# Hybrid S5 and pooling layer on one core: every queue position set anew, a head with identity transposes and halved loads

## The chip, the cores and the metric

The kernel runs on one core of one Trainium2 chip. The metric is the device time of one execution in microseconds (us); lower is better. The time before is 720.16 us, the median of three runs (717.47 to 720.93).

## The reference

One decoder layer over a prompt of 2048 tokens and 8 single-token samples, model width 1024. Cut to what matters:

```python
proj = h @ w_in                                  # 1024 -> 2048
s_in, s_gate, p_in, p_gate = jnp.split(proj, [512, 1024, 1536], axis=-1)
sy, hr, hi = _s5_mixer(s_in, ...)                # complex diagonal scan, 32 groups x 64 states
sy = gelu(sy)
sy = sy * sigmoid(sy @ glu_w + glu_b)
py, buf = _pool_mixer(p_in, ...)                 # trailing means over 2, 4, 8, 16 tokens, then a 128x128 map each
mixed = concat([sy * silu(s_gate), py * silu(p_gate)])
y = _layer_norm(alpha * h + mixed @ w_out, ln_g, ln_b)
```

All tensors are 32-bit floats. The kernel keeps the precision by splitting each matmul operand into a high and a low part (`hl`), so that a product takes three matmuls: high by high, and the two mixed ones.

## The kernel before, in words

All of the work sits in one function, `hybrid_step`. The tokens are worked in chunks of 512, 512, 512, 256 and 256 (plus the 8 samples); for the first two column blocks the chunks are finer (256, 256, 512, 512, 256, 256).

**Stages.** (1) The head: `load_x`/`put_x` (lines 506 and 522) load 128 tokens, transpose them on TensorE (8 transposes, line 147) into PSUM, ScalarE casts them to the high part `xh` (line 156) and VectorE subtracts for the low part `xl` (line 150). Two PSUM pairs (tag `pair`) take turns. `load_w`/`split_w` (lines 174 and 180) load and split 128 columns of `w_in`. (2) `proj(m, c)` (line 196) multiplies column block m (0 to 15) by a chunk: 24 matmuls into one bank. Blocks 0 to 3 are the SSM input (`u_tile`, line 533), 4 to 7 its gate, 8 to 11 the pooling input, 12 to 15 the pooling gate. (3) Beside it `params` (line 222) works out the SSM's constants from small loads: a long chain of short VectorE instructions, then eight rounds of two groups each in which VectorE forms the products `sp`, TensorE multiplies and transposes into `ps_ks`, and the results go to DRAM (`sw_d`, `qw_d`, `wt_d`). `tables` (line 460) builds rotation tables in four quarters, each of six doubling levels, four `tx` pairs and two stores; a quarter's tile must be stored before the next one's first memset. (4) `ssm_task` (line 662) runs 16 groups: rotate, scan, rotate back on VectorE, and short matmuls on TensorE; the outputs go to `y_d` in DRAM. (5) The pooling blocks: `pool_in`, `pool_diff` (adds on GpSimd, a difference `df` on VectorE, its split `dh`) and `pool_gate` with the matmuls `pm`. (6) `prep` reads `y_d` back and splits it (`yh`), `glu_chunk` multiplies by the GLU weights (line 1060), `out_tile` by `w_out` (line 1100), and the layer norm ends each 128 tokens; `out_last` is the last tile and has its own tail.

**What sets the order.** TensorE, ScalarE, VectorE and GpSimd are under a manual schedule (line 495): each engine runs its instructions in the order in which the program emits them. That order comes from the class `Line` (line 47). Its clock `line.t` is advanced by the planned TensorE time of the matmuls that are emitted (3n/2400 for three matmuls of n columns). Tasks are generators: where one says `yield 3.0`, it goes on when `line.t` has come 3.0 further, and what it then issues lands in the engines' queues between the matmuls emitted before and after. `line.finish(task)` jumps the clock forward until the task is done. So every `yield` number is a place in the queues and no wait on the chip; a number too small puts an instruction in front of others while its inputs are still missing, and the engine stands. SyncE's queue, which issues all DMAs, follows the same program order and waits for each DMA's inputs.

The places that the steps below touch: `PD` (line 544), the start of `params`; `PY` and `YS` (lines 490 and 491), the yields of a round of constants and of an SSM group; `x_task` (line 563), which puts the token tiles from the fourth on; `ssm_tail` (line 919), which starts when the SSM is done, and the `hook` (line 1016) that adds it at the second step of pooling block 11; the delays of `w_task` and `w_in_task` (lines 185 and 192).

## Time and profile before

| what | value |
|---|---|
| median of three runs | 720.16 us |
| the profiled execution: its own time | 722.89 us |
| its span, first to last instruction | 721.1 us |
| TensorE busy | 685.0 us, 95% |
| VectorE busy | 483.1 us, 67% |
| ScalarE / GpSimd busy | 237.2 / 189.2 us |
| mean granted TensorE clock | 0.984 |

The profile is one execution. "Busy" counts the time in which an engine had an instruction in work; the time that TensorE wasn't busy, about 36 us, is what a new order can give back, besides stretches at the lower clock. A row of a timeline gives the start, the duration and the number of merged instructions; in brackets stands the idle time of the engine before it and what ended it.

### The profile page before, as it was taken

Reading aid. Unit: us, or ns where it says so; the run is one execution under the profiler, and the core shown is the slowest. Engines: PE = TensorE matmul, PEld = TensorE weight load, DVE = VectorE, ACT = ScalarE, POOL = GpSimd, SP = SyncE. Lnnn points to the kernel's source line nnn. Section 1 sums busy time; section 2 is a strip of 40 time slices with the busy share of each in tenths; the row PEclk is TensorE's granted clock in tenths of the full one; section 3 lists DMA queues with packets and bytes.
Section 4 is the critical chain, followed back from the end, with each engine's and each line's share of the span. In section 5 each row is a group of like instructions: output and inputs, shape, how many; then the busy total and the mean of one; then the engine's idle time right before and its main releaser. Section 6 shows DMA issues by size and latency. Waiting matters only on the chain.

```text
span 721.1 us, 10754 instructions
## 1 busy us (share of the span) xinstructions
PE 685.0 (95%) x3735; PEld 579.2 (80%) x3735; DVE 483.1 (67%) x999; ACT 237.2 (33%) x487; POOL 189.2 (26%) x251
## 2 busy tenths in 40 slices
PE   6999997999999999999998999989999999999995
PEld 5988785887888888988986787777888868888884
DVE  3689969754466788789788853487554556656444
ACT  4343323322344443443433221254221323323100
POOL 1005534410000011121222313646313233151322
PEclk9999998999999999999999999999999999999998
DMA  8993675777645545354443224935455563634432
GB/s 278 231 336 91 163 202 146 178 187 221 195 149 159 166 116 154 126 155 146 138 146 114 81 67 134 322 113 125 113 118 129 136 159 78 148 88 117 116 88 59
DMA packets 137909, 107.95 MB, mean 150 GB/s; under 512 B 74435, under 2 KB 115559, under 8 KB 137847
## 3 DMA queue, kind: packets, MB, share of 16 engines
q1 hardware_dynamic: 137855, 107.27, 53.2%
q8 instruction: 29, 0.48, 0.3%
q14 instruction: 25, 0.20, 0.1%
HBM read 64.74 MB, written 42.73 MB: 149 GB/s over the span
## 4 chain that ended last, share of the span: by engine, by line
PE 65%; DVE 6%; ACT 3%; POOL 2%; issue 2%; DMA 1%; SPq 1%; DVEq 0%; ACTq 0%; POOLq 0%
PE pj L208 29%; PE o L1100 24%; PE z L1060 5%; POOL ws L150 2%; PE y L653 2%; PE s L638 2%; PE y L723 1%; PE pm L864 1%; PE os L1100 1%; DVE mix L150 1%; DMA wst<-in_w_in_dram 1%; SPq L456 1%; DVE sp L150 0%; DVE wo L150 0%; DMA wt<-wt_d 0%
## 5 line engine op out<-in xcount | busy, mean ns | idle before, releaser
L208 PE MATMUL pj<-xh,w 128*128 128x512 f32 (+2 forms) x1312 | 337.5, 350 | 1.7 <-ACT w L156 1.7
L208 PEld LDWEIGHTS pj<-xh,w 128*128 128x128 f32 x1312 | 226.5, 192 | 31.6 <-ACT w L156 1.9
L208 PE MATMUL pj<-xl,w 128*128 128x512 f32 (+2 forms) x656 | 208.4, 349 | 0.0
L1100 PE MATMUL o<-wo,mix 128*128 128x512 f32 (+1 forms) x792 | 176.0, 383 | 0.8 <-ACT mix L156 0.8
L1100 PEld LDWEIGHTS o<-wo,mix 128*128 128x128 f32 x792 | 145.3, 188 | 30.6 <-ACT mix L156 1.1
L208 PEld LDWEIGHTS pj<-xl,w 128*128 128x128 f32 x656 | 121.1, 191 | 15.5
L150 POOL TENSOR_TENSOR ws<-pc 128x527 f32<-128x527 f32 (+1 forms) x20 | 19.8, 992 | 120.9 <-ACT pc L815 72.2
L150 POOL TENSOR_TENSOR xr<-xr,gb 128x1024 f32<-128x1024 f32 x15 | 36.0, 2398 | 48.8 <-DVE xr L150 43.5
L1060 PE MATMUL z<-yh,w_g 128*128 128x512 f32 (+2 forms) x240 | 46.7, 355 | 0.0
L1060 PEld LDWEIGHTS z<-yh,w_g 128*128 128x128 f32 x240 | 39.9, 193 | 6.4
L1089 ACT ACTIVATE xr<-xr,mv 128x1024 f32<-128x1024 f32 x15 | 18.7, 1244 | 79.7 <-DVE mv L1079 74.4
L1068 DVE SCALAR_TENSOR_TENSOR xr<-xr,o 128x512 f32<-128x512 f32 (+1 forms) x33 | 22.0, 667 | 26.0 <-PE o L1100 26.0
L150 POOL TENSOR_TENSOR ws<-ws 128x525 f32<-128x525 f32 (+5 forms) x30 | 35.7, 1190 | 3.8 <-DVE dh L150 1.7
L697 POOL COPY bus<-SP 128x16 f32<-128x16 f32 x16 | 6.6, 415 | 112.4 <-ACT SP L691 109.8
L150 DVE TENSOR_TENSOR xl<-pt,xh 128x1024 fp32r<-128x1024 f32 (+1 forms) x17 | 19.8, 1164 | 16.3 <-ACT xh L156 16.1
L775 DVE SCALAR_TENSOR_TENSOR g<-g,pj 128x512 f32<-128x512 f32 (+1 forms) x20 | 11.6, 580 | 28.3 <-ACT g L774 28.3
L150 POOL TENSOR_TENSOR mv<-mv,mhalf 128x1 f32<-128x1 f32 x16 | 9.9, 617 | 74.0 <-DVE mv L1074 66.3
L150 DVE TENSOR_TENSOR yh<-y,yh 128x512 fp32r<-128x512 f32 (+2 forms) x20 | 12.2, 610 | 22.1 <-ACT yh L156 22.1
L150 DVE TENSOR_TENSOR mix<-y,mix 128x512 fp32r<-128x512 f32 (+2 forms) x20 | 18.2, 912 | 12.1 <-ACT mix L156 12.1
L150 DVE TENSOR_TENSOR xr<-xr,gb 128x1024 f32<-128x1024 f32 x15 | 18.3, 1221 | 10.5 <-ACT xr L1089 10.5
L156 ACT CAST hh<-hf 128x528 fp32r<-128x528 f32 x16 | 10.1, 634 | 45.9 <-DVE hf L150 42.9
L156 ACT CAST xh<-pt 128x1024 fp32r<-128x1024 f32 (+1 forms) x17 | 16.4, 966 | 24.9 <-PE pt L147 24.9
(220 smaller groups left out, 892.9 us busy)
## 6 DMA issues: line engine op xcount, KB each, us to landing
wst<-in_w_in_dram SPq DMA_DIRECT2D x16, 512.0 KB
xr<-in_x_prompt_dram SPq DMA_DIRECT2D x24, 256.0 KB
out_dram<-xr SPq DMA_DIRECT2D x22, 256.0 KB
xw<-in_x_prompt_dram SPq DMA_DIRECT2D x8, 512.0 KB
wt_d<-wzero SPq DMA_DIRECT2D x4, 1024.0 KB
sw_d<-sv SPq DMA_DIRECT2D x8, 512.0 KB
qw_d<-qh SPq DMA_DIRECT2D x16, 256.0 KB
ws<-sw_d SPq DMA_DIRECT2D x16, 256.0 KB
```

The source lines that it names most:

```text
L150: (eng or V).tensor_tensor(out=out, in0=a, in1=b, op=op)
L156: S.copy(out=hi, in_=src)
L208: nc.tensor.matmul(out=ps[:, :n], lhsT=w[:, a, k], rhs=xcols(b, k, t0, n), start=(i == 0), stop=(i == 23))
L456: dma(out=wt_d[j, :, :, gs, :, 16 * j:P].rearrange("a c g h o -> (a c) (g h) o"), in_=kv[:, :, :, 0:P - 16 * j].rearrange("p g h o -> p (g ...
L638: nc.tensor.matmul(out=ps[:, c, 0:264], lhsT=ws[:, c, a], rhs=uh[:, b, c, 8:272], start=(i == 0), stop=(i == 2))
L653: nc.tensor.matmul(out=py[:, c, 0:264], lhsT=wq[cs, r, a], rhs=hh[cs, b, r], start=False, stop=(i == 5))
L723: nc.tensor.matmul(out=py[:, c, 0:264], lhsT=wt[:, c, a], rhs=uh[:, b, c, 0:264], start=(i == 0), stop=False)
L775: V.scalar_tensor_tensor(out=g[:, :n], in0=g[:, :n], scalar=1.0, in1=jm(ps[:, :n]), op0=ALU.add, op1=ALU.mult)
L1060: nc.tensor.matmul(out=ps[:, :n], lhsT=w[:, a, k, P * (m % 2):P * (m % 2) + P], rhs=yh[:, b, k, :n], start=(i == 0), stop=(i == 11))
L1068: V.scalar_tensor_tensor(out=xt[:n, c], in0=xt[:n, c], scalar=ALPHA, in1=ps, op0=ALU.mult, op1=ALU.add)
L1089: S.activation(out=xt[:n], in_=xt[:n], func=AF.Identity, scale=mv[:n, 2:3], bias=mv[:n, 0:1])
L1100: nc.tensor.matmul(out=ps, lhsT=lhs(a, k), rhs=wo_view(k)[:, b, 512 * h + c.start:512 * h + c.stop], start=(i == 0), stop=(i == len(hl) * ...
```

## The change

Nothing is computed otherwise. Three kinds of edit:

1. The head. `load_w` and `split_w` can work in parts; the first weights come in two parts; the second token tile is loaded in halves, as the first was; the second weights are loaded ahead of the fourth token tile and split only after the first product tile; 12, 8 and 8 identity transposes whose results nobody reads are put before the first, between the first two and after the second token tile; the third token tile moves from the head into `x_task`; the first product tiles take the order high-high, high weight by low tokens, low weight.
2. About 60 yields, delays and pauses get other numbers (some only another spelling: 0.5 to 0.50).
3. The last tile's first half is stored from ScalarE's queue.

The diff, cut to its core:

```diff
-    def w_task(src, key, delay=4.0):
+    def w_task(src, key, delay=1.77):
...
-            order = [(k, a, b) for a, b in ((0, 0), (1, 0), (0, 1)) for k in range(KT)]
+            order = [(k, a, b) for a, b in (HL if t0 == 0 else ((0, 0), (1, 0), (0, 1))) for k in range(KT)]
...
-        yield 0.5
+        yield 0.00
         def expo(out, z, shape, nm):
...
-            yield 3.2
+            yield 3.77
...
-                yield 2.08
+                yield 1.38
...
-            yield 0.5
+            yield 0.00
         pw = tmp.tile([P, 2, GP, 9], F32, name="pw")
...
     def tables():
         while "table" not in ready or "x" not in ready:
-            yield 0.5
+            yield 0.58
...
-                yield (1.12, 0.8, 0.8, 1.0, 1.4, 2.2)[lv]
+                yield (1.20, 0.71, 0.79, 1.00, 0.74, 2.20)[lv]
...
-    YS = (1.25, 1.5, 1.4, 1.0, 1.8, 0.8, 1.1, 1.2)
-    PY = (5.0, 3.0, 2.2)
+    YS = (1.25, 1.50, 1.40, 1.00, 3.02, 0.80, 1.10, 1.04)
+    PY = (5.08, 3.00, 2.20)
...
-        split(pv[:, :, :n], hi, lo)
+        if i < 2:
+            for k in range(0, KT, 4):
+                split(pv[:, k:k + 4, :n], hi[:, k:k + 4], lo[:, k:k + 4])
+        else:
+            split(pv[:, :, :n], hi, lo)
...
+    def busy(n):
+
+        ps = pair("busy")
+        for i in range(n):
+            transpose(ps[:, i % 2, 0:P], ident, P)
+
-    PD = 0.5
+    PD = 1.36
     load_x(0)
     load_x(1)
-    st0 = load_w(wi[:, 0:P], 0)
+    st0 = load_w(wi[:, 0:P], 0, parts=2)
     load_x(2)
+    st1 = load_w(wi[:, P:2 * P], 1, prod, "hl")
     load_x(3)
-    st1 = load_w(wi[:, P:2 * P], 1, prod, "hl")
+    busy(12)
     put_x(0)
     load_x(4)
-    split_w(st0, 0)
+    busy(8)
     put_x(1)
     load_x(5)
-    put_x(2)
-    load_x(6)
-    split_w(st1, 1, G)
+    busy(8)
+    split_w(st0, 0, parts=2)
     line.t = 0.0
...
-        for i in range(3, 17):
+        for i in range(2, 17):
...
-            yield 2.88
+            yield 2.88 if i > 2 else 1.10
...
-    xg = line.add(x_task(), 0.38)
+    xg = line.add(x_task(), 0.80)
...
         for m in range(2):
+            if m and c[0] == 0:
+                split_w(st1, 1, G)
             u_tile(m, c)
...
-    w3 = line.add(w_in_task(3, 3.0))
+    w3 = line.add(w_in_task(3, 2.48))
...
-    line.add(w_in_task(4, 3.0))
+    line.add(w_in_task(4, 1.12))
...
         while any(x[1] in (par, tab) for x in line.tasks):
-            yield 0.5
+            yield 0.09
...
-        yield 12.0
+        yield 10.44
         ssm_uh(0)
...
-            yield 1.4
+            yield 1.46
             yield YS[3]
...
-        yield 0.9 + 1.04 * (len(bin(w)) - 3) * n / 512
+        yield 0.98 + 1.22 * (len(bin(w)) - 3) * n / 512
...
         while any(x[1] is sg for x in line.tasks):
-            yield 0.35
+            yield 0.37
...
-        yield 7.0 if ck else 15.0
+        yield 5.43 if ck else 13.90
...
-            yield 1.0 if ck else 6.72
+            yield 2.70 if ck else 6.72
...
-                yield 1.3
+                yield 3.60
...
-            yield 3.22 if h else 1.12
+            yield 4.12 if h else 1.12
...
-        yield 0.5
+        yield 0.84
         V.scalar_tensor_tensor(out=gs[:, :n], in0=ps[:, :n], scalar=1.0, in1=gs[:, :n], op0=ALU.add, op1=ALU.mult)
-        yield 0.5
+        yield 0.66
...
-    def ln_store(yout, ot, n, c):
+    def ln_store(yout, ot, n, c, q=dma):
         for j in range(len(yout)):
-            dma(out=yout[j][:, c], in_=ot[j * n // len(yout):(j + 1) * n // len(yout), c])
+            q(out=yout[j][:, c], in_=ot[j * n // len(yout):(j + 1) * n // len(yout), c])
...
-        yield 1.5
+        yield 0.99
         tt(xt[:n], xt[:n], gb[:n, 0], ALU.mult)
-        yield 1.0
+        yield 0.67
...
-            ln_store(yout, xt, P, c)
+            ln_store(yout, xt, P, c, dma if c.start else S.dma_start)
```

## Rows read from the trace of the kernel before

**Rows 1.** The page, part 1: busy time of each engine.

```profile
PE 685.0 (95%) x3735; PEld 579.2 (80%) x3735; DVE 483.1 (67%) x999; ACT 237.2 (33%) x487; POOL 189.2 (26%) x251
```

**Rows 2.** Waits of TensorE over the span: in total, times, longest.

```profile
PE ps_ks L147 <- DVE sp L150: 9.8, 6, 4.7
...
PE pm L864 <- ACT dh L156: 3.8, 4, 1.4
PE s L638 <- DVE uh L150: 2.6, 2, 1.4
PE pj L208 <- ACT w L156: 1.7, 1, 1.7
```

**Rows 3.** Windows: busy of PE, PEld, DVE, ACT, POOL; PEclk; DMA share; GB/s.

```profile
74.00:75.00 1.00, 1.00 (x6) 1.00 (x7) 1.00 (x2) 0.00 (x0) 1.00 (x2) 0.50 0.00 0
...
77.00:78.00 1.00, 1.00 (x9) 1.00 (x9) 0.77 (x4) 1.00 (x5) 0.00 (x0) 0.89 0.91 177
...
166.00:169.00 3.00, 3.00 (x13) 2.85 (x14) 2.12 (x6) 1.20 (x3) 0.00 (x0) 0.50 0.77 273
```

**Rows 4.** The timeline of the head: start, duration, engine, line, operation.

```profile
8.00 1.97 PE L147 MATMUL pt<-ident,xst 128*128 128x128 f32 x8 [2.35 <-DMA xst<-in_x_prompt_dram]
9.71 1.04 ACT L156 CAST w<-wst 128x1024 fp32r<-128x1024 f32 x1 [3.01 <-DMA wst<-in_w_in_dram]
...
12.69 1.63 PE L208 MATMUL pj<-xh,w 128*128 128x256 f32 x6
...
14.06 1.04 ACT L156 CAST w<-wst 128x1024 fp32r<-128x1024 f32 x1
...
17.97 1.03 PE L147 MATMUL pt<-ident,xst 128*128 128x128 f32 x8
...
18.76 2.15 PE L208 MATMUL pj<-xh,w 128*128 128x256 f32 x16
```

**Rows 5.** The timeline of VectorE and TensorE, 66 to 107 us.

```profile
66.38 0.86 DVE L150 TENSOR_TENSOR mt<-tb,zs 128x64 f32<-128x64 f32 x2
...
69.82 3.11 DVE L150 TENSOR_TENSOR sp<-bbar,prv 128x256 f32<-128x256 f32 x4
...
73.44 1.28 PE L147 MATMUL ps_ks<-ident,sp 128*128 128x128 f32 x4 [2.46 <-DVE sp L150]
...
84.31 0.76 DVE L150 TENSOR_TENSOR sp<-sp,sp 128x256 f32<-128x256 f32 x2
...
86.92 0.66 PE L147 MATMUL ps_ks<-ident,sp 128*128 128x128 f32 x4
...
99.08 2.99 DVE L482 SCALAR_TENSOR_TENSOR tx<-tb,zs,ms 128x64 f32<-128x64 f32 x6
...
106.88 0.06 DVE L466 MEMSET tb<- 128x4 f32 x1 [4.21 <-DMA tb_d<-tb]
```

**Rows 6.** The timeline of SyncE's queue, ScalarE and TensorE, 149 to 167 us.

```profile
149.14 4.54 SPq L456 DMA_DIRECT2D wt_d<-kv  x8
...
159.13 1.05 ACT L156 CAST w<-wst 128x1024 fp32r<-128x1024 f32 x1 [4.67 <-DMA wst<-in_w_in_dram]
...
165.99 1.24 PE L147 MATMUL ps_ks<-ident,sp 128*128 128x128 f32 x4 [1.41 <-DVE sp L150]
```

**Rows 7.** The timeline around the SSM's end, 381 to 454 us.

```profile
381.88 0.62 ACT L156 CAST dh<-df 128x512 fp32r<-128x512 f32 x1 [5.36 <-DVE df L150]
...
427.95 1.04 ACT L156 CAST w<-wst 128x1024 fp32r<-128x1024 f32 x1
...
429.65 0.37 SPq L951 DMA_DIRECT2D y<-y_d  x1
...
453.53 0.62 ACT L156 CAST yh<-y 128x512 fp32r<-128x512 f32 x1
```

**Rows 8.** The timeline at the end of the pooling stage: TensorE.

```profile
482.43 0.98 PE L864 MATMUL pm<-dh,pw_sb 128*128 128x264 f32 x3 [1.37 <-ACT dh L156]
```

**Rows 9.** The timeline of SyncE's queue at the end of the kernel.

```profile
716.11 2.39 SPq L1083 DMA_DIRECT2D out_dram<-xr  x4
```

More of the change, by code (lines that the diff above doesn't have):

```diff
@@ L172, in hybrid_step, with load_w, split_w @@
     wtiles, wpend, ready, shared = {}, {}, {}, {}
-    def load_w(src, key, pool=None, tag="wst"):
+    def load_w(src, key, pool=None, tag="wst", parts=1):
         st = (pool or wst).tile([P, KT * P], F32, tag=tag, name=f"wst_{key}")
         k = src.shape[0] // P
-        dma(out=st.rearrange("p (k c) -> p k c", k=k), in_=src.rearrange("(k p) c -> p k c", p=P))
+        kp = k // parts
+        for i in range(0, k, kp):
+            dma(out=st.rearrange("p (k c) -> p k c", k=k)[:, i:i + kp], in_=src[P * i:P * (i + kp)].rearrange("(k p) c -> p k c", p=P))
         return st
-    def split_w(st, key, eng=None):
+    def split_w(st, key, eng=None, parts=1):
         w = wpool.tile([P, 2, KT * P], F32R, tag="w", name=f"w_{key}")
-        split(st, w[:, 0], w[:, 1], eng)
+        n = KT * P // parts
+        for i in range(0, KT * P, n):
+            split(st[:, i:i + n], w[:, 0, i:i + n], w[:, 1, i:i + n], eng)
         wtiles[key] = w
-    def w_task(src, key, delay=4.0):
+    def w_task(src, key, delay=1.77):
         yield from l_wst.get()
@@ L249, in params @@
         transpose(ps[:, 64:72], ng, 8)
-        yield 0.8
+        yield 0.80
         lam = tmp.tile([P, 3, GP], F32, name="lam")
@@ L362, in params @@
         tt(q1, q1, den, ALU.mult)
-        yield 1.0
+        yield 1.00
         m1 = prod.tile([P, 2, GP, CH], F32, tag="p1", name="bm1")
@@ L402, in params @@
         q_products(0)
-        yield 5.5
+        yield 5.50
         kv = None
@@ L423, in params @@
             while not tabs:
-                yield 0.5
+                yield 0.50
             ps = pair("ps_ks")
@@ L677, in ssm_task @@
         ps = ssm_s(0)
-        yield 0.59
+        yield 0.51
         ph = bank("ps_h0")
@@ L682, in ssm_task @@
         S.copy(out=hs0.rearrange("p a b g -> p (a b g)"), in_=ph[:, 0:256])
-        yield 2.4
+        yield 2.40
         prev = None
@@ L718, in ssm_task @@
                     yield YS[2]
-            yield 0.8
+            yield 0.80
             py = pair(f"y{gp}")
@@ L752, in ssm_task @@
         tt(hsn, hsn, bus, ALU.add)
-        yield 6.0
+        yield 5.86
         ssm_out(*prev)
@@ L794, in pool_setup @@
         dma(out=o_pool_s[0, :, 0:14, :], in_=state_pool[0, :, 1:15, :])
-        yield 5.0
+        yield 4.50
         split(pst, pw_sb[:, 0], pw_sb[:, 1])
@@ L852, in pool_diff @@
         l_diff.free()
-        yield 2.4
+        yield 2.40
         dfs[gi, t0] = dh
@@ L866, in pool_gate @@
         line.t += 0.64 * n / 512
-        yield 1.0
+        yield 1.00
         sl = gbT[:, 4 + gi:5 + gi]
@@ L881, in step_now @@
             pass
-    sg = line.add(ssm_task(), 0.5)
+    sg = line.add(ssm_task(), 0.50)
     gt = pw_sb = rcnt = sps = None
@@ L890, in hybrid_step @@
             sps = gt.tile([P, 4, NB], F32, name="sps", bufs=1)
-            line.add(pool_setup(), 0.0)
+            line.add(pool_setup(), 0.00)
         nxt = (6, 7, 8, 12)[m]
@@ L1003, in wo_a @@
         wo_load(0, 0, 2, 6)
-        yield 7.0
+        yield 7.00
         yield from wo_split(1, (0, 1, 2, 3))
@@ L1010, in mix_a @@
                   mixes[0][:, 0, 4 + m, :], mixes[0][:, 1, 4 + m, :], G if m % 2 else V)
-            yield 0.85
+            yield 0.83
     stage = []
@@ L1030, in g1_task @@
         while "g1" not in ready:
-            yield 0.3
+            yield 0.28
         split_w(st, "g1")
@@ L1063, in glu_chunk @@
                 line.go(3 * n / 2400.0)
-            last = line.add(glu_tail(ck, m, ps, yt[:, m]), 0.0)
+            last = line.add(glu_tail(ck, m, ps, yt[:, m]), 0.00)
         return last
@@ L1119, in out_tile @@
             ln_part(xt, ps, st[:, h], P, slice(512 * h, 512 * h + 512))
-        line.add(ln_tail(xt, st, P, yout, nm), 0.0)
+        line.add(ln_tail(xt, st, P, yout, nm), 0.00)
     def sample_in(mix, c0):
@@ L1139, in out_sample @@
             ln_part(xt, ls, st[:, h], NB, c)
-        line.add(ln_tail(xt, st, NB, [y_sample.rearrange("b l d -> (b l) d")], "s"), 0.0)
+        line.add(ln_tail(xt, st, NB, [y_sample.rearrange("b l d -> (b l) d")], "s"), 0.00)
     def out_last(mix, c0, xin, yout, nm):
@@ L1160, in hybrid_step @@
     wb = line.add(wo_split(0, (6, 7, 0, 1)))
-    mb = line.add(mix_a(), 0.5)
+    mb = line.add(mix_a(), 0.54)
     gl = glu_chunk(0)
-    preps = {1: line.add(prep(1), 3.0)}
+    preps = {1: line.add(prep(1), 3.11)}
     line.finish(wb)
@@ L1182, in hybrid_step @@
             new_mix(ck + 1)
-            pp = line.add(prep_pool(ck + 1), 1.0)
+            pp = line.add(prep_pool(ck + 1), 1.24)
         mix = mixes.pop(ck)
@@ L1195, in hybrid_step @@
                 if ck + 2 < len(CHUNKS):
-                    preps[ck + 2] = line.add(prep(ck + 2), 3.0)
+                    preps[ck + 2] = line.add(prep(ck + 2), 2.32)
         if more:
```

43 lines of the change are left out of this document (21 added, 22 removed).

## The prediction

> **What bounds it now.** I read the busy times first: TensorE has work for 685.0 of 721.1 us [rows 1], so no edit can be worth more than the 36 us in which it stands, plus what its lower clock costs. Then its waits [rows 2]: the largest is not for a DMA but for VectorE's products `sp` in the rounds of constants (9.8 us in six waits), then for the pooling's `dh` (3.8), the SSM's `uh` (2.6) and one weight cast (1.7). The windows show what each long wait costs again afterwards: the granted clock is 0.50, the lower level of 1.2 GHz, after the engine stood, and full again some us later [rows 3]. The timelines then say why VectorE, ScalarE or a store was late [rows 4 to 9]. From about 520 to 713 us TensorE has no wait in the list; nothing can be won there. So the question at each place is: which instruction stands in a queue in front of the one that TensorE needs, and do the new numbers move it?
>
> I follow the planned clock of the program by adding up yields; "planned" marks such a time. It runs slightly fast: an SSM group has 12.25 planned us (YS plus 0.8 and 1.4).
>
> **The change part by part.**
>
> *The head.* Before, the second token tile's transposes start at 8.00 when its load lands, the first weights are cast at 9.71, the first product matmul starts at 12.69, and the second column block at 18.76 with tiles 0 to 4 transposed [rows 4]. Eight transposes take 1.97 early and 1.03 once the engine has been at work [rows 4]. The identity is made on the chip and waits for no load, so 12 + 8 + 8 transposes nearly fill TensorE until the loads land; I take it that tile 1 then costs 1.03, not 1.97, ending near 9.1. ScalarE then needs about 1.0 for tile 1 and 1.04 for the weights, in halves, so the first product can start near 11.0 (an estimate), 1.7 earlier. But tile 2 now comes inside it (1.03), tile 3 lands later, where the second weights were (they were cast at 14.06 [rows 4], so 13.8 at best): its transposes end near 14.8 and the last 12 of the 24 matmuls near 16.2. And here the moved `split_w(st1)` bites: ScalarE copies the product out and only then casts the second weights (1.04 [rows 4]), while TensorE has nothing else in its queue. The second block starts near 17.7 (an estimate, the copy at under half of the cast), with one tile fewer (tile 4, 1.03): 18.8 against 18.76. I count the head at 0. Bounds: -1.5 if that cast is covered, +2 if the clock isn't raised (below). The two added DMA issues and the halved casts lie beside loads that land later anyway. GpSimd's low part of the second weights, needed only by matmuls 17 to 24, is covered by the others; without that it would cost about 1.
>
> *The rounds of constants, 60 to 145 us.* VectorE is the limit here: it is busy nearly without a gap from 66 to 77 and TensorE waits 2.46 for the first round's `sp` [rows 5]. In the queue before `sp` stand two doubling levels of the table (66.38 to 69.82: 3.4 us [rows 5]), which nobody needs before the SSM. By the yields, `params` issues its first `sp` 0.73 planned us earlier (PD +0.86; -0.07, -0.50, 2 x 0.27, -0.09, +0.27, -0.70, 2 x -0.50, -0.04), and the product tiles come 0.9 later, since tile 2 now counts on the line. `x_task` ends 1.52 later, so the table starts 1.3 later. Its fourth and fifth levels so fall behind `sp`: 3.4 us less in front of it, while TensorE arrives 1.6 earlier. The 2.46 go, and with them half of the some 3.7 us at 0.50 that follow (73.4 to 77.1, [rows 3]): 1.85. That is 4.3. Not all is kept: VectorE's work is the same and TensorE reaches the next rounds sooner. At the second round it had 1.85 to spare (86.92 against `sp` ended at 85.07 [rows 5]), at the third it waits already, and before the third three `tx` pairs now stand instead of one (99.08: six in 2.99 [rows 5], so two more pairs, four instructions, are 2.0). Further on stands the worst wait, 4.7 [rows 2]: VectorE stands 4.21 in the memset of the third quarter, whose tile isn't stored yet [rows 5], and new numbers (6.0 to 6.00) leave that distance alone. So I keep 2.5 of the 4.3. Bounds: 0 and -8 (if that wait goes too).
>
> *The last round, 164 us.* ScalarE stands 4.67 for weights whose load SyncE could issue only after eight stores of `kv` (4.54) [rows 6]; everything behind it is late, TensorE stands 1.41 [rows 6] and then runs 3 us at 0.50 [rows 3], which costs 1.5. The stores come 1.15 earlier against the tiles (-0.73 + 6 x 0.08 - 0.9), the load with them: -1.5 of 2.9. Bounds: 0 and -2.9.
>
> *The SSM.* Its group gets 13.37 planned us instead of 12.25 (YS +1.22 and -0.16, +0.06): 17.9 over 16 groups, less 1.56 + 0.4 + 0.1 at the start. It spreads the same VectorE work over more matmuls. TensorE's waits for `uh` (2.6 [rows 2], at 386 and 402 us) begin with ScalarE standing 5.36 in front of a `dh` whose `df` isn't there [rows 7]; with `df` issued 0.44 later (0.08 + 2 x 0.18) and VectorE less crowded I take a little over half, -1.5. Bounds: +1 and -3. What it moves past: the end of the SSM slides some 16 us, so the reads of `y_d`, issued from 429.65, go to about 446, and the first `yh`, at 453.53 before [rows 7], waits behind them with 7 us left where it had 24. I count 0.
>
> *The weights of block 15.* Their cast starts at 427.95 [rows 7], after the last gate's two ScalarE steps, and TensorE stands 1.7 [rows 2]. The split is due 6.4 planned us after its load is asked for; the two tiles between have 5.2, plus 0.66 (an SSM matmul group) plus 0.32: 6.18 at the last place, just short. With the SSM later two such groups fall there: 6.84. The cast goes ahead of the gate: -1.5. Bounds: 0 and -1.7.
>
> *The pooling's end, 448 to 483 us.* GpSimd's adds take longer than planned, so `pm` stands in TensorE's queue before `dh` is there (3.8 [rows 2]; the last one 1.37 [rows 8], followed by the lower clock). With four adds the yield is 5.86 for 5.06: 0.8 more matmuls go first. The last, where the line jumps, stays. -1.5; bounds 0 and -5.
>
> *The tail.* Four stores are issued one after another, 2.39 [rows 9]: 0.6 each. With two on ScalarE's idle queue the last is issued about 0.6 earlier; -0.6, bounds +0.3 and -1.2.
>
> The weights of blocks 3 and 4 (2.48, 1.12) and the later numbers of the output stage have no TensorE wait to remove; earlier casts there make ScalarE wait for a load, covered by its idle time (237.2 busy [rows 1]); uncovered they cost a us.
>
> **Sum:** 0 - 2.5 - 1.5 - 1.5 - 1.5 - 1.5 - 0.6 = -9.1. Against the profiled execution, 722.89 (span 721.1 and 1.8 around it), that is 713.8; that execution stands 0.4% above the median of the runs, 720.16, so in terms of the median **711**.
>
> **The rivals.**
>
> *Transposes don't raise the clock.* For it: the early transposes ran at 0.25 each, and full speed came only once product matmuls had started [rows 4]; the rows can't say which of the two brought it. Then 28 of them take 7 us at the low rate, tile 1 ends near 10.5 and the first product starts near 12.7 without tile 2 (1.97): +2. The time: 713. Trainium skill, "TensorE: Matmul & The Clock Gate", Part 4: PE-mode transpose: a transpose doesn't count as work for the clock gate in the way a matmul does. By that rule this rival holds; the trace neither confirms nor refutes it.
>
> *VectorE falls further behind (slower).* A quarter of the table takes 15.04 planned us instead of 15.72 (the levels lose 0.68), so the same VectorE work is asked for beside less TensorE work, in a stretch that is bound by it. Place: `sp` of the rounds from the second on. It decides when TensorE, ahead by 1.6, comes to the second round more than 1.85 before `sp` ends. Price: the first wait only moves (0 instead of -2.5), two rounds more wait about 2.5 with 1.85 of clock each (8.7), the worst wait grows by 1.7 (0.7 and a level of about 1), the last round's gain is lost; with the other gains (-5.1): +5.3, so 725. Against it: the two levels behind `sp`.
>
> *All is handed back.* The first wait's gain is lost at the third round, the last round keeps its wait, the others bring half: -2.9, so 717, no change that can be told. For it: nothing of VectorE's work is removed.
>
> *The jam clears.* The memset's wait of 4.21 shrinks too, since the table's stores come 2.3 planned us earlier; that wait of 4.7 goes with a clock loss like the one at 74 (1.85), and the rest of the SSM's and the pooling's waits (1.1 and 2.3): 9.9 on top of 9.1, so 701. Against it: the store still follows the same SyncE queue.
>
> **How the numbers follow.** Forecast 0.46 (711), no clock from transposes 0.12 (713), handed back 0.18 (717), VectorE behind 0.12 (725), jam clears 0.12 (701). A measurement of this kernel can tell about 0.5%, 3.6 us, from no change: below 716.6 is faster, 0.70; between 716.6 and 723.8 the same, 0.18; above, slower, 0.12. The range of the forecast alone is 704 to 717 by the bounds; 702 to 722 takes in the handed-back case and leaves out most of the two ends.
>
> **What would show it.** Right: no wait before the first `ps_ks` transposes and no 0.50 near 74; transposes of tile 1 in about 1.0; the second block's weights cast after the first copy, with a TensorE gap of 1 to 1.5 near 16.5; no wait of 1.7 at block 15; `yh` not waiting for `y_d`. Wrong: waits for `sp` that add up to 9.8 or more, or ScalarE standing for `y_d`.

## The result and the profile after

The changed kernel takes **710.9 us**, the median of four runs (709.68 to 713.83), beside 718.82 of the kernel before in the same comparison (717.41 to 720.93): ratio 0.9893, 95% interval 0.985 to 0.9937, so faster by about 1.1%. Six more runs later gave 711.55 (707.72 to 712.27), ratio 0.9881, interval 0.9851 to 0.9911. Each beside its own kernel before, the gain is 7.9 us (718.82 - 710.90) and 7.5 (719.01 - 711.55). The profiled execution took 713.83 with a span of 711.9; it stands 0.4% above its median, as the one of before did, so the two traces may be laid side by side: 722.89 - 713.83 = 9.06 us.

The busy times of the changed kernel, for [rows 1]:

```profile
PE 684.9 (96%) x3763; PEld 580.3 (82%) x3763; DVE 490.4 (69%) x1002; ACT 237.3 (33%) x490; POOL 194.3 (27%) x251
```

TensorE's waits, for [rows 2] (total, times, longest, in us):

```profile
PE ps_ks L147 <- DVE sp L150: 6.6, 5, 2.4
PE pm L880 <- ACT dh L156: 3.3, 3, 1.9
PE pj L212 <- ACT w L156: 2.6, 2, 1.4
PE pt L147 <- DMA xst<-in_x_prompt_dram: 2.1, 1, 2.1
PE o L1116 <- ACT mix L156: 1.5, 2, 0.7
```

Gone are the wait of 4.7 for `sp`, those for `uh` and the 1.7 of block 15; new are one of 2.1 for a token tile near 46 us and a second one for `mix` (the split inputs of the last matmuls; before, it was one of 0.8); the pooling's has hardly changed. `pj` for `w` is now the head's.

To see where the 9.06 us arise I laid the traces side by side **by work done**: each matmul counts with what its shape takes at full clock (the lower quartile of the distance from its start to the next matmul's, over the traces compared; identity transposes count nothing), and each line of the table compares the times at which a kernel's TensorE had done equal work. Negative is earlier than before. The last four kernels are the experiments below. The columns are profiles of single executions. That of the kernel before, 722.89, stands some 3 us above its medians, and every column but the first is of an execution within 1.5 us of its own median; so some 3 us of their leads are that one execution's, and they are best compared with each other. The rows from 379 to 437 hold to about 0.9, by what the SSM's short matmuls, which overlap, are counted at.

| before, us | changed | control | old head | old SSM | old pooling | before, two `tb` |
|---|---|---|---|---|---|---|
| 32.1 | -0.3 | -0.8 | -0.2 | -0.2 | -0.9 | -0.3 |
| 42.2 | 0.0 | -0.4 | -0.2 | +0.4 | -0.9 | -0.3 |
| 52.4 | +2.3 | +0.5 | -0.1 | +1.3 | +0.5 | -0.3 |
| 88.0 | +2.1 | +0.4 | +0.1 | +0.9 | +0.3 | -0.4 |
| 109.9 | +4.9 | +3.2 | +2.0 | +2.8 | +1.6 | -0.8 |
| 128.3 | -3.3 | -5.0 | -5.0 | -5.4 | -6.6 | -9.0 |
| 174.1 | -3.5 | -6.6 | -7.5 | -4.2 | -8.3 | -9.2 |
| 379.2 | -3.8 | -6.9 | -7.7 | -3.1 | -8.6 | -9.3 |
| 403.9 | -7.6 | -10.7 | -11.1 | -3.6 | -12.9 | -9.3 |
| 437.0 | -10.0 | -13.1 | -13.6 | -3.9 | -15.3 | -9.2 |
| 470.5 | -12.4 | -15.4 | -16.4 | -7.1 | -17.0 | -9.2 |
| 483.3 | -10.5 | -13.6 | -13.9 | -4.8 | -15.9 | -9.2 |
| 496.1 | -12.1 | -15.2 | -15.5 | -6.5 | -16.5 | -10.8 |
| 507.6 | -9.1 | -12.0 | -13.5 | -4.4 | -16.1 | -7.8 |
| 698.4 | -9.1 | -11.6 | -13.5 | -4.4 | -16.1 | -7.8 |

So nothing is won up to 42 us, 2.3 us are lost near 46 (0.9 in the control), nothing comes back at the first round, 2.8 are lost at the third (+2.1 to +4.9), 8.2 are won at one place at 110 to 128 us (+4.9 to -3.3), 0.2 at the last round (1.6 in the control), 3.8 and 2.4 in the SSM's last groups and at block 15, and another 2.4 up to 470. Of these 1.9 are gone again at 483.3, where the first GLU matmul `z` starts in the kernel before, and 1.4 are handed back at the first output.

**The head.** TensorE's timeline of the changed kernel, for [rows 4]:

```profile
7.49 1.09 PE L147 MATMUL pt<-ident,xst 128*128 128x128 f32 x8
11.12 1.26 PE L212 MATMUL pj<-xh,w 128*128 128x256 f32 x8 [1.21 <-ACT w L156]
17.55 0.98 PE L212 MATMUL pj<-xh,w 128*128 128x256 f32 x6 [1.41 <-ACT w L156]
18.37 1.03 PE L147 MATMUL pt<-ident,xst 128*128 128x128 f32 x8
```

Tile 1's transposes run at the full rate before any product has started, the first product is 1.57 earlier, the second weights' cast then costs 1.41, and tile 4 comes at 18.37 (17.97 before).

**The rounds of constants.** VectorE and TensorE of the changed kernel, for [rows 5], then SyncE's queue before and after:

```profile
62.14 1.22 DVE L150 TENSOR_TENSOR xl<-pt,xh 128x1024 fp32r<-128x1024 f32 x1
69.68 3.46 DVE L150 TENSOR_TENSOR sp<-bbar,prv 128x256 f32<-128x256 f32 x4
74.12 0.88 PE L147 MATMUL ps_ks<-ident,sp 128*128 128x128 f32 x4 [2.35 <-DVE sp L150]
106.54 0.06 DVE L470 MEMSET tb<- 128x4 f32 x1
```

```profile
96.63 4.47 SPq L456 DMA_DIRECT2D wt_d<-kv  x7
101.64 1.23 SPq L486 DMA_DIRECT2D tb_d<-tb  x2
```

```profile
94.90 0.91 SPq L490 DMA_DIRECT2D tb_d<-tb  x2
98.44 4.48 SPq L460 DMA_DIRECT2D wt_d<-kv  x7
```

The fourth and fifth levels do stand behind `sp` now, yet `sp` starts at 69.68 where it started at 69.82: a token tile's `xl` (62.14) has moved in front of it, VectorE had stood for the tiles that came late near 46 us, and short instructions ahead of the table are slower (the mask 0.64 for 0.15, a copy 0.58 for 0.16); the first three levels take 3.7 to 3.8 us in both. TensorE's wait is 2.35 for 2.46. In the control, which waited only 0.69 for that tile, `sp` starts at 67.91 and is done 1.1 us earlier than before, TensorE comes 1.0 earlier, and its wait is 2.36. But the memset of the third quarter finds its tile stored (no bracket; 4.21 before): its stores were issued at 94.90, ahead of the seven `kv` stores, where they stood behind them, at 101.64.

**The last round and the SSM's end**, for [rows 6, 7]: ScalarE's cast and TensorE at the last round, the cast of block 15's weights, the first `yh`, and SyncE's reads of `y_d`:

```profile
155.51 1.05 ACT L156 CAST w<-wst 128x1024 fp32r<-128x1024 f32 x1 [2.18 <-DMA wst<-in_w_in_dram]
160.26 1.24 PE L147 MATMUL ps_ks<-ident,sp 128*128 128x128 f32 x4 [1.73 <-DVE sp L150]
415.93 1.03 ACT L156 CAST w<-wst 128x1024 fp32r<-128x1024 f32 x1
443.16 0.62 ACT L156 CAST yh<-y 128x512 fp32r<-128x512 f32 x1
436.88 3.85 SPq L967 DMA_DIRECT2D y<-y_d  x4
```

ScalarE stands 2.18 for 4.67, but TensorE still 1.73 for 1.41 (1.79 in the control). Block 15's cast is in time, and `yh` doesn't stand for `y_d`, whose reads slid by 7 us.

**The pooling's end and the first output**: TensorE before, then after (for [rows 8]), and the granted clock of the changed kernel (first column after the window: TensorE busy; the clock is PEclk, third from the end):

```profile
483.33 12.77 PE L1060 MATMUL z<-yh,w_g 128*128 128x512 f32 x48
501.80 1.47 PE L1100 MATMUL o<-wo,mix 128*128 128x512 f32 x4 [0.75 <-ACT mix L156]
```

```profile
471.98 0.97 PE L880 MATMUL pm<-dh,pw_sb 128*128 128x264 f32 x3 [1.87 <-ACT dh L156]
472.87 11.16 PE L1076 MATMUL z<-yh,w_g 128*128 128x512 f32 x48
489.36 1.23 PE L1116 MATMUL o<-wo,mix 128*128 128x512 f32 x3 [0.75 <-ACT mix L156]
491.33 16.03 PE L1116 MATMUL o<-wo,mix 128*128 128x512 f32 x62 [0.75 <-ACT mix L156]
```

```profile
77.00:78.00 1.00, 1.00 (x6) 1.00 (x6) 0.97 (x3) 0.00 (x0) 0.58 (x1) 0.50 0.00 0
161.00:163.00 2.00, 2.00 (x11) 2.00 (x10) 0.73 (x2) 0.84 (x2) 0.00 (x0) 0.50 0.91 320
473.00:484.00 11.00, 11.00 (x49) 9.09 (x50) 10.59 (x11) 7.23 (x12) 7.67 (x4) 1.00 0.65 182
492.00:495.00 3.00, 3.00 (x8) 2.37 (x8) 1.38 (x3) 0.00 (x0) 0.00 (x0) 0.50 0.34 55
```

From the first `z` to the end of the last wait for `mix` it is 18.47 us before (501.80 - 483.33) and 18.46 after (491.33 - 472.87): a chain on VectorE and ScalarE sets it, whatever TensorE does (18.3 to 18.5 in eight of the profiles below). Before, the low clock fell into `z` (12.77), where this chain hides it. After, `z` runs at full clock (11.16), TensorE is early, stands twice, and the clock falls to 0.50 behind the chain, where nothing hides it; that is the 1.4 above. The change isn't what moved it: the kernel before with two `tb` (below), whose steps here are all the old ones, has `z` at full clock and waits twice for `mix` as well:

```profile
474.15 11.15 PE L1060 MATMUL z<-yh,w_g 128*128 128x512 f32 x48
```

The clocks at 77 and 161 us are the 0.50 of [rows 3] again.

### The profile page after: what moved, and what is told of

The parts are those of the page before. It is cut to its first block, busy times and chain, and to the rows that moved or that the text cites. A ratio compares the mean times of both kernels' runs of the same rounds, so it can differ in the third digit from the quotient of the medians.

```text
span 711.9 us, 10836 instructions
## 1 busy us (share of the span) xinstructions
PE 684.9 (96%) x3763; PEld 580.3 (82%) x3763; DVE 490.4 (69%) x1002; ACT 237.3 (33%) x490; POOL 194.3 (27%) x251
## 4 chain that ended last, share of the span: by engine, by line
PE 71%; DVE 7%; ACT 3%; DMA 2%; SPq 2%; issue 1%; DVEq 0%; POOL 0%; ACTq 0%; POOLq 0%
PE pj L212 34%; PE o L1116 24%; PE z L1076 5%; PE y L669 2%; PE y L739 2%; PE s L654 2%; PE pm L880 1%; SPq L460 1%; PE os L1116 1%; DVE tx L486 1%; DMA wst<-in_w_in_dram 1%; DVE mix L150 1%; DVE wo L150 1%; DMA u_d<-ue 1%; DVE sp L150 1%
## 5 line engine op out<-in xcount | busy, mean ns | idle before, releaser
L1116 PE MATMUL o<-wo,mix 128*128 128x512 f32 (+1 forms) x792 | 178.2, 386 | 1.5 <-ACT mix L156 1.5
L212 PEld LDWEIGHTS pj<-xl,w 128*128 128x128 f32 x656 | 121.7, 192 | 15.3
L1076 PE MATMUL z<-yh,w_g 128*128 128x512 f32 (+2 forms) x240 | 45.1, 347 | 0.0
L713 POOL COPY bus<-SP 128x16 f32<-128x16 f32 x16 | 8.6, 535 | 119.9 <-ACT SP L707 119.8
L150 POOL TENSOR_TENSOR ws<-ws 128x525 f32<-128x525 f32 (+5 forms) x30 | 34.0, 1133 | 3.3 <-DVE dh L150 1.1
L150 DVE TENSOR_TENSOR xl<-pt,xh 128x1024 fp32r<-128x1024 f32 (+2 forms) x19 | 20.0, 1057 | 20.7 <-ACT xh L156 20.6
L150 DVE TENSOR_TENSOR yh<-y,yh 128x512 fp32r<-128x512 f32 (+2 forms) x20 | 13.9, 693 | 23.5 <-ACT yh L156 23.5
L707 ACT COPY SP<-s 64x264 f32<-64x264 f32 x64 | 23.9, 373 | 17.3 <-PE s L654 16.8
L791 DVE SCALAR_TENSOR_TENSOR g<-g,pj 128x512 f32<-128x512 f32 (+1 forms) x20 | 11.6, 578 | 23.5 <-ACT g L790 23.5
L150 DVE TENSOR_TENSOR xr<-xr,gb 128x1024 f32<-128x1024 f32 x15 | 19.7, 1314 | 10.5 <-ACT xr L1105 10.5
L156 ACT CAST xh<-pt 128x1024 fp32r<-128x1024 f32 (+2 forms) x19 | 16.7, 884 | 26.4 <-PE pt L147 24.9
```

Source lines behind the costliest of these rows:

```text
L150: (eng or V).tensor_tensor(out=out, in0=a, in1=b, op=op)
L156: S.copy(out=hi, in_=src)
L212: nc.tensor.matmul(out=ps[:, :n], lhsT=w[:, a, k], rhs=xcols(b, k, t0, n), start=(i == 0), stop=(i == 23))
L707: S.copy(out=SP[64 * c:64 * c + 64, a], in_=ps[64 * a:64 * a + 64, c, 0:264])
L791: V.scalar_tensor_tensor(out=g[:, :n], in0=g[:, :n], scalar=1.0, in1=jm(ps[:, :n]), op0=ALU.add, op1=ALU.mult)
L1076: nc.tensor.matmul(out=ps[:, :n], lhsT=w[:, a, k, P * (m % 2):P * (m % 2) + P], rhs=yh[:, b, k, :n], start=(i == 0), stop=(i == 11))
```

## The experiments

Two questions: which edit brought which part of the table, and whether the terms that stayed at zero are at zero for the reason given. The times in brackets are the lowest and the highest run.

**The old head (old head).** The head of the kernel before in the changed kernel.

```diff
-    busy(12)
     put_x(0)
...
+    split_w(st0, 0)
...
+    put_x(2)
...
+    split_w(st1, 1, G)
```

> The changed kernel (710.9 us) with the head of the kernel before; all other positions stay new. Theory A (the head acts through SyncE's queue): with the old head the table's stores of the second quarter stand behind the seven kv stores again, so VectorE's memset for the third quarter waits 3 to 4.5 us for a store near 103 to 107 us and TensorE waits 4 us or more for the third or fourth sp; in exchange the wait of 2.1 us for a token tile near 46 us is gone. The two together were worth 3.25 us between 42 and 128 us, so the time is 713 to 715 us. Theory B (the new positions of the table and the parameters cleared the jam): no wait for a store at the memset, only the 2.3 us at 46 us are won, the time is 708 to 709.5 us.

710.42 (708.99 to 711.56), ratio 0.9881, interval 0.9854 to 0.9907: the head is worth nothing that can be told. Neither theory holds as stated. The queue of A is there, its wait isn't; SyncE, then VectorE:

```profile
96.30 4.48 SPq L460 DMA_DIRECT2D wt_d<-kv  x7
100.82 1.00 SPq L490 DMA_DIRECT2D tb_d<-tb  x2
```

```profile
104.39 0.06 DVE L470 MEMSET tb<- 128x4 f32 x1
```

The stores stand behind the `kv` stores as before, but the memset has moved behind the round's `diag`, `kv` and `qh` on VectorE, comes at 104.39 and not at 102.67, and finds them landed.

**The old constants.** All yields of `params`, `tables` and `PY` as before, the rest new.

```diff
-                yield (1.20, 0.71, 0.79, 1.00, 0.74, 2.20)[lv]
+                yield (1.12, 0.8, 0.8, 1.0, 1.4, 2.2)[lv]
...
-    PY = (5.08, 3.00, 2.20)
+    PY = (5.0, 3.0, 2.2)
```

> The changed kernel (710.9 us) with the old positions inside the parameters, the table and the rounds of constants (their yields); the head and all the rest stay new. Theory A (the head acts through SyncE's queue): the second quarter's table stores still stand ahead of the kv stores, no wait at the memset, and the time stays at 710 to 712.5 us. Theory B (these positions cleared the jam): the memset waits 3 to 4.5 us again, TensorE's waits for sp sum to 9 us or more (6.6 in the changed kernel), and the time is 716 to 720 us.

711.92 (710.99 to 712.39), ratio 0.9901, 0.9877 to 0.9925. As A said: the memset comes at 102.56, where it came before, and doesn't wait, since the stores are issued ahead of the `kv` stores (at 94.07). TensorE's first wait for `sp` is 4.07 here and all of them come to 8.0, under B's 9; the time is the changed kernel's all the same. With the run above: the jam has **two keys**, the place of the stores in SyncE's queue and that of the memset in VectorE's, and either alone opens it. A's other half, that the head alone does it, has fallen.

**The old SSM (old SSM).** `YS` and the yields at the SSM's start and end as before.

```diff
-    YS = (1.25, 1.50, 1.40, 1.00, 3.02, 0.80, 1.10, 1.04)
+    YS = (1.25, 1.50, 1.40, 1.00, 1.80, 0.80, 1.10, 1.20)
...
```

> The changed kernel (710.9 us) with the old positions of the SSM's groups (YS, the start, the end). Theory A: it is the longer group that removed TensorE's waits for uh and the wait for the weights of block 15; both come back (1 to 3 us of waits for uh near 375 to 400 us, 1 to 1.8 us for block 15's weights near 418 us), and with the lower clock behind them the time is 714.5 to 717.5 us. Theory B: those waits were a matter of when the SSM starts, and go with the 3.3 us by which TensorE is earlier at 170 us; the time stays within 1.5 us of 710.9.

717.55 (715.3 to 720.27), ratio 0.9963, 0.9941 to 0.9986: these yields alone are worth about 5 to 7 us (5.0 by the two ratios, 6.7 by the medians, 717.55 - 710.9). Without them the change brings 0.37%, less than the second buffer of the next experiment alone (0.63%). TensorE waits again:

```profile
383.95 0.51 PE L669 MATMUL y<-hh,wq 64*128 64x264 f32 x4 [1.27 <-ACT hh L156]
425.11 0.50 PE L212 MATMUL pj<-xh,w 128*128 128x512 f32 x1 [1.71 <-ACT w L156]
```

The 1.7 at block 15 is back; the other wait is now for the SSM's `hh` instead of `uh`. A holds, in all but that name, the time at the upper end of its range.

**Two buffers for the table (before, two `tb`).** The kernel before, nothing else changed.

```diff
-            tb = tabs[0].tile([P, 2, 4, HT], F32, tag="tb", name=f"tb{q}")
+            tb = tabs[0].tile([P, 2, 4, HT], F32, tag="tb", name=f"tb{q}", bufs=2)
```

> The kernel before (718.8 us) with a second buffer for the table's tile, so that the memset of a quarter needn't wait for the store of the quarter ahead of it; nothing else changes. Theory A: the 4.21 us of the memset and TensorE's wait of 4.7 us for sp behind it go, with the clock that it costs some 8 us at most, part of it handed back later: 711 to 714 us. Theory B (VectorE's work is the limit of this stretch, so a wait of it only moves): TensorE's waits for sp still sum to 8 us or more of 9.8 and the time is 717 us or above.

714.71 (713.55 to 715.12), ratio 0.9937, 0.9916 to 0.9958: the jam costs about 4.5 us of 719 (0.63%), 7.8 in the profiled executions. VectorE, then TensorE:

```profile
102.19 0.06 DVE L466 MEMSET tb<- 128x4 f32 x1
```

```profile
122.44 0.92 PE L147 MATMUL ps_ks<-ident,sp 128*128 128x128 f32 x4 [1.77 <-DVE sp L150]
```

The memset's wait is gone, a part comes back as 1.77 at a later round, and all the rest of the old kernel's waits stand. A, a little short.

**The zeros behind the token loads.** The four 1 MB stores of zeros made to depend on token tile 12.

```diff
-        G.memset(z.bitcast(F32), 0.0)
...
+                S.mul(z.bitcast(F32), xT[0][1][:, 0:4, 512:640].bitcast(F32), 0.0)
```

> The changed kernel (710.9 us) with the four stores of 1 MB of zeros made to wait for token tile 12 (the zeros come from ScalarE as that tile times zero), so that they are issued behind all token loads. Theory A (the new head lets two of these stores ahead of tile 12's load on a DMA that is nearly full): no wait for a token tile near 46 us (2.1 us in the changed kernel's profile, 0.6 in two others with the same loads), TensorE 0.6 to 2.3 us earlier at 60 us; the time is 708.5 to 710.5 us. Theory B (VectorE sets the pace from 60 us on): the 46 us wait goes and the first wait for sp grows by as much; the time stays within 1 us of 710.9.

710.83 (708.54 to 712.48), ratio 0.9872, 0.9835 to 0.9909: no change. The wait at 46 us is gone, but it was only 0 to 1.4 in the eight other profiles with the new head (control 0.69). Of the 2.1 us in the changed kernel's profile most was that execution's own. The time is as Theory B said; the first wait for `sp` is 2.68.

**The table behind the first `sp`.**

```diff
+            ready["sp"] = True
...
-        while "table" not in ready or "x" not in ready:
+        while "table" not in ready or "x" not in ready or "sp" not in ready:
```

> The changed kernel (710.9 us) with the table started only when the first sp is in VectorE's queue: three doubling levels (65.85 to 69.68, 3.8 us) leave the front of it. Theory A (those levels are what keeps the first sp late): the wait of 2.35 us before the first ps_ks transposes falls under 0.5 and the granted clock stays near 1.00 at 74 us; half is handed back in the next rounds, 707.5 to 709.5 us. Theory B (VectorE's work only moves): the sum of the waits for sp stays at 6 us or more, and the time within 1.5 us of 710.9 or above it.

712.36 (711.64 to 712.61), ratio 0.9892, 0.9858 to 0.9926. The first wait goes at last, and TensorE is 3.4 us ahead of the kernel before at 77.6, where it was 0.9 behind at 52; then the second round takes it all (2.3 behind at 88):

```profile
85.15 0.47 PE L147 MATMUL ps_ks<-ident,sp 128*128 128x128 f32 x1 [2.96 <-DVE sp L150]
```

That isn't the end of it. At the third round TensorE doesn't stand at all (2.2 us in the control), and at 128 us it has gained 7.7 since 52 us, the control 5.5: some 2.2 us are kept. Then the jam is back, a quarter later. SyncE, VectorE, TensorE:

```profile
119.07 3.89 SPq L461 DMA_DIRECT2D wt_d<-kv  x7
123.50 0.59 SPq L491 DMA_DIRECT2D tb_d<-tb  x1
127.82 0.06 DVE L471 MEMSET tb<- 128x4 f32 x1 [2.98 <-DMA tb_d<-tb]
137.57 0.33 PE L147 MATMUL ps_ks<-ident,sp 128*128 128x128 f32 x1 [3.74 <-DVE sp L150]
```

One of the third quarter's two `tb` stores has slipped behind the seven `kv` stores, and the memset of the fourth quarter stands for it. The waits for `sp` sum to 8.3. The numbers are Theory B's, the reason only in part: one round hands the gain back, the next returns about half, and what keeps the time where it was is the jam.

**The splits on VectorE.** What GpSimd splits ahead of the first output goes to VectorE.

```diff
-            split(stage[0][:, at[k]], w[:, k, 0], w[:, k, 1], G if k % 2 and not h else V)
+            split(stage[0][:, at[k]], w[:, k, 0], w[:, k, 1], V)
...
-                  mixes[0][:, 0, 4 + m, :], mixes[0][:, 1, 4 + m, :], G if m % 2 else V)
+                  mixes[0][:, 0, 4 + m, :], mixes[0][:, 1, 4 + m, :], V)
```

> The changed kernel (710.9 us) with the four splits that GpSimd makes beside VectorE ahead of the first output matmuls (two of wo, two of mix) given to VectorE. Theory A (the two engines slow each other: mix took 2.30 each beside GpSimd and 0.69 alone, wo 2.31 and 1.22): VectorE does all eight in 7.6 us instead of its share in 8.1, the last mix is ready 0.5 us earlier after z starts than the 18.46 us of both kernels, TensorE's two waits of 0.75 shrink and less clock is lost at 492 us: 709 to 710.5 us. Theory B (VectorE's queue is full and simply gets more work): the last mix is ready later, the waits for mix grow to 3 us or more, 712 us or above.

708.21 (706.72 to 710.94), ratio 0.9842, 0.9805 to 0.9879: below the range of Theory A. The interval overlaps those of the changed kernel, so the 2.7 us of the medians are likely and not certain. VectorE of the changed kernel, then of this one:

```profile
476.44 4.60 DVE L150 TENSOR_TENSOR mix<-stage,mix 128x512 fp32r<-128x512 f32 x2
480.96 2.31 DVE L150 TENSOR_TENSOR wo<-stage,wo 128x1024 fp32r<-128x1024 f32 x1
```

```profile
474.63 1.29 DVE L150 TENSOR_TENSOR mix<-stage,mix 128x512 fp32r<-128x512 f32 x2
475.83 1.22 DVE L150 TENSOR_TENSOR wo<-stage,wo 128x1024 fp32r<-128x1024 f32 x1
```

Eight splits take VectorE 6.95 us alone (471.76 to 478.71), four beside GpSimd took it 7.89 (475.30 to 483.19), and the chain from the first `z` to the last `mix` is 16.72 us (486.04 - 469.32) for 18.46. The Trainium skill ("SBUF — State Buffer", Who interferes with whom) says that a VectorE instruction with two inputs in SBUF contends with a GpSimd instruction that reads SBUF; these rows agree, 2.30 for 0.65 each.

**Without the identity transposes.**

```diff
-    busy(12)
...
-    busy(8)
```

> The changed kernel (710.9 us) without the 28 transposes of the identity. Theory A (they raised the clock before any product matmul had run): tile 1's transposes take 1.9 to 2.0 us instead of 1.09, the first product matmul starts 0.7 to 1.2 us later than 11.12, and up to 1 us of it is still there at 40 us. Theory B (the loads' landing sets the start of the first product): tile 1 again in 1.9 to 2.0, but the first product within 0.3 us of 11.12 and nothing left at 20 us.

One run, 709.03. TensorE:

```profile
10.52 2.08 PE L212 MATMUL pj<-xh,w 128*128 128x256 f32 x8 [2.54 <-ACT w L156]
12.61 1.91 PE L147 MATMUL pt<-ident,xw 128*128 128x128 f32 x8
```

The first product starts within the spread of those with them (9.92 to 11.20), but runs at the low rate (2.08 for 1.26), and so does the next tile (1.91 for 1.03). At 32 us TensorE is 1.0 us behind the kernel before, where the ten profiles with them lie 0.1 to 1.1 ahead of it: they are worth 1.1 to 2.1 us there. Theory A by its size, not by its place. At 128 us, behind the rounds that VectorE paces, it is 4.3 ahead of the kernel before, in the midst of those (3.3 to 7.1), and the one time shows no loss.

**The control.** The changed kernel again.

> The changed kernel once more, as a control. In its first profile it waited 2.1 us for a token tile near 46 us and twice 0.75 for mix at 489 and 491 us, and its time was 713.83 where its other runs were 709.7 to 711.2. Theory A: these two are chance of one execution (five of the runs since, with the same loads, waited 0 to 0.9 us at 46 us), so the median is 709.5 to 711 and a profile of a run near it shows neither in full. Theory B: they belong to the change; both stand again, and the median is 712 or more.

711.55; see the result. The wait at 46 us shrank to 0.69, the two of 0.75 for `mix` stood again: half A, half B. Its column shows 3 us more lead at 174 us than the first profile, from that wait and the last round, where its clock stayed at 1.00: so much can lie between two executions.

**The old pooling (old pooling).** The yields behind GpSimd's adds as before.

```diff
-        yield 0.98 + 1.22 * (len(bin(w)) - 3) * n / 512
+        yield 0.9 + 1.04 * (len(bin(w)) - 3) * n / 512
...
-        yield 4.50
+        yield 5.0
```

> The changed kernel (710.9 us) with the old positions of the pooling's steps after GpSimd's adds (and of the pooling's first step). Theory A (the last wait for dh and VectorE's chain behind it set the time of the first output matmuls, so what the other gates wait doesn't count): the waits for dh change by up to 1 us, the time by less than 1 us: 710 to 712. Theory B (the term of my sum): the later positions saved 1.5 us, so 712 to 713 us.

**707.06** (706.66 to 708.35), ratio 0.9829, 0.9797 to 0.9861: 4.5 us less than the control on the same chip, and the fastest of all. Neither theory foretold that. TensorE:

```profile
466.32 1.28 PE L880 MATMUL pm<-dh,pw_sb 128*128 128x264 f32 x3 [2.22 <-ACT dh L156]
467.39 12.22 PE L1076 MATMUL z<-yh,w_g 128*128 128x512 f32 x48
485.69 17.55 PE L1116 MATMUL o<-wo,mix 128*128 128x512 f32 x75 [0.75 <-ACT mix L156]
```

The waits for `dh` are no shorter (3.4 for 3.3 in all), but the low clock lies in `z` again, only one wait for `mix` is left, and the first output ends 2.8 us further ahead of the control than it began (-16.1 to -12.0, from -16.5 to -15.2). Another 1.7 of the lead was there at 174 us; up to there every queue holds the control's instructions in the control's order, so that part lies between two executions of the same work. Four other profiles with the new pooling yields had the low clock in `z` as well (old constants, zeros, late table, no identity transposes), and one with the old yields had it behind (before, two `tb`), so the yields don't fix where it falls in an execution. The fastest run of the control took 707.72. How much of the 4.5 belongs to the yields stays open.

**The window adds on VectorE**, for the last two pieces, with the copy ahead of them.

```diff
...
-            tt(nx[:, lo:16 + n], cur[:, lo:16 + n], cur[:, lo - d:16 + n - d], ALU.add, G)
+            tt(nx[:, lo:16 + n], cur[:, lo:16 + n], cur[:, lo - d:16 + n - d], ALU.add, V if gi == 3 and n == 256 else G)
```

> The changed kernel (710.9 us) with the window adds of the last two pooling pieces (four adds each of 256 columns, and the copy of 16 columns ahead of them) on VectorE instead of GpSimd, which took 5.0 us from that copy's end to the last add for the last piece. Theory A: VectorE does the four in about 1.7 us, the last dh is there 2.5 us or more earlier, the wait of 1.87 us before the last pm goes and VectorE's chain to the first output starts earlier with it: 708 to 709.5 us. Theory B (VectorE is as full there, its other work moves back by as much): 710.5 us or above, with longer waits for dh or mix elsewhere.

711.95 (710.65 to 712.61), ratio 0.9892, 0.9859 to 0.9924: Theory B. The adds end early and the difference still comes late:

```profile
465.23 1.38 DVE L150 TENSOR_TENSOR ws<-ws 128x269 f32<-128x269 f32 x3
469.31 0.42 DVE L849 SCALAR_TENSOR_TENSOR df<-ws,pc 128x256 f32<-128x256 f32 x1
```

Between them VectorE makes a `yh`, a `y`, a `gp` and a `wo` of other tasks, put there by the yield that was sized for GpSimd. The adds were moved, `df` wasn't.

**The adds and the splits on VectorE, the glu tails interleaved.**

```diff
...
-        yield 0.66
+        yield 0.66 if ck else 2.90
         split(gs[:, :n], mix[:, 0, m, :n], mix[:, 1, m, :n])
```

> The changed kernel (710.9 us) with both: the adds of the last two pooling pieces and the four splits ahead of the first output on VectorE, and the steps of the four glu tails of the first chunk interleaved, so that VectorE makes the next y while ScalarE casts the mix of the one before (VectorE stands 0.69 four times there). If the parts add up: 710.9 - 2.7 (splits, as measured) - 2 (adds) - 1 (tails) = 705 us, and no wait for mix above 0.3; if the chain to the first output is the only limit that all three relieve, 706 to 708 us.

708.46 (706.83 to 710.53), ratio 0.9854, 0.9824 to 0.9884. No wait for `mix` is left, but the time is that of the splits alone: the parts don't add up. Its median and that of the old pooling lie 2.4 to 4.5 us below those of the changed kernel, with intervals that overlap the control's (0.9851 to 0.9911); the two together weren't tried.

## Why the prediction was right, and where it was not

The time (711.0 for 710.9), the sign and the range hold. Of the seven terms one holds as it was put, two in their mechanism but not their size, and the others fail in mechanism, sign or size. The sum held because their errors cancel, and that is luck; so is the last microsecond, since 711 was reckoned from 720.16 and the kernel before took 718.82 beside the changed one: 7.9 us were won where 9.1 were forecast. Of the signs of being right the first failed (a wait of 2.35 before the first `ps_ks`, 0.50 at 77 us), and the other four stand.

- **The head, 0: right, with its steps.** Tile 1 at the full rate (1.09), the second block's gap of 1.41 at 17.55, 0.0 at 42 us; with the old head the time is the same. What it overlooked lies behind: a wait for a token tile near 46 us, 0 to 2.1 us in the profiles with the new loads. The rival that transposes don't raise the clock has fallen: tile 1 took 1.09 before any product, and the run without them starts its products at half the rate. (Only the durations tell this: the granted clock reads 1.00 from the start in all these traces, also where eight transposes took 1.97.) The Trainium skill ("TensorE: Matmul & The Clock Gate", Part 4: PE-mode transpose) says that the full clock doesn't engage for transposes. By that rule tile 1 would have taken about 1.97; it took 1.09, and the measurement decides.
- **The rounds of constants, -2.5: within its bounds, the mechanism wrong.** From 52 to 128 us both profiles of the changed kernel gain 5.5 to 5.6. The step that failed: "Its fourth and fifth levels so fall behind `sp`: 3.4 us less in front of it", so "The 2.46 go". They fall behind it, but I didn't count what moves in front, and by my own terms 2.46 - 3.4 + 1.6 leaves 0.7; in the control `sp` is done 1.1 earlier and TensorE comes 1.0 earlier, so the wait stands at 2.36. The share that I kept, 2.5 of 4.3, isn't refuted: with the whole table behind `sp` some 2.2 us were left two rounds on. What was won instead is the wait behind the memset: "new numbers (6.0 to 6.00) leave that distance alone" was the second failed step. It is the jam of my rival "the jam clears", at 8.2 us in the profiles (2.8 had been lost at the third round just ahead of it) and 4.5 by the run with two buffers. Against it I held that "the store still follows the same SyncE queue". It doesn't: one loop of the source issues both `tb` and `tx` stores, and in the changed kernel the seven `kv` stores stand between the two. SyncE isn't among the engines of the manual schedule (line 495), and its order came out otherwise when other things moved; the text ahead of the prediction, by which its queue follows the program's order, is wrong there.
- **The last round, -1.5: wrong.** ScalarE's wait halved as foreseen (2.18), but `sp` was later than the weights, and TensorE's wait grew (1.73, 1.79 in the control). The 1.5 of lower clock that I counted behind it belongs to an execution: the clock stayed at 1.00 there in the control, and after the old wait of 1.41 in the kernel before with two `tb`.
- **The SSM, -1.5, and block 15, -1.5: right in mechanism, too small.** The longer group removed the waits for `uh` and `w`; the table gives -3.8 and -2.4, the run with the old numbers 5 to 7 in all. The mis-sized term is "a little over half" of the waits: all went. TensorE stands 3.1 us between 379 and 404 us before and 0.25 after, 1.7 and 0 at block 15. No lower clock is in it: the granted clock of the kernel before reads 1.00 from 379 to 437 us. Counting 0 for `y_d` was right.
- **The pooling's end, -1.5: wrong.** From 437 us to the first `z` (483.3) the changed kernel gains 0.5, the kernel with the old pooling 0.6. The step that failed: "0.8 more matmuls go first". They do, the wait at the last piece stays all the same (1.87), and what counts is the 18.46 us of VectorE and ScalarE behind it, which I hadn't looked for, since TensorE showed one wait of 0.75 there. Behind `z` 1.4 are lost again (1.6 in the control, nothing with the old pooling) by where the low clock falls.
- **The tail, -0.6: too large.** From the last matmul's end to the end of the span it is 8.4 us before (721.1 - 712.72) and 8.2 after (711.9 - 703.65). The last store is issued 0.6 earlier as foreseen (done 5.2 us after the last matmul for 5.8), but the span then lasts another 3.1 for 2.6.
- **VectorE further behind** has not come about: the waits for `sp` sum to 6.6.

## What to carry to other kernels

Before a wait is counted as won, list what moves in front of the instruction as well as what moves behind it, and on a stretch that one engine paces expect part of the gain to be handed back a round later unless that engine's work or one of its own waits goes (here all of it at the next round, some 2.2 of 4.3 us left two rounds on). A queue that no one orders by hand can come out in another order after any edit (the jam left at the third quarter and was back at the fourth in one run), so a store that blocks a buffer needs a second buffer, not a lucky place. And see where a lower clock falls: under a longer chain of other engines it cost nothing here, right behind that chain 1.4 to 1.6 us.
